# First 60 gathered u rows free of TensorE's pace, gate and spill loads issued from POOL

## The chip, the cores and the metric

One core of a Trainium2 chip runs the whole kernel in one launch. The metric is the device time of one execution in microseconds. Five engines take part: TensorE (PE in the profile, its weight loads PEld), VectorE (DVE), ScalarE (ACT), GpSimd (POOL) and SyncE (SP), which here only issues transfers.

## The reference

The model is two transformer blocks on 512 tokens of 1024 features in f32. The part that matters is the feed-forward layer of the first block's first layer, in which each token picks 8 x 16 = 128 of 16384 experts:

```python
def peer_ffn(x, w_q, sub_keys, u_emb, v_emb):
    ...
        eidx = jnp.take_along_axis(cidx, pos, axis=-1)      # 128 experts per token
        gate = jax.nn.softmax(top_s, axis=-1)
        u = u_emb[eidx]
        hid = jax.nn.gelu(jnp.einsum('td,thkd->thk', xc, u))
        wgt = (gate * hid.astype(jnp.float32)).astype(xc.dtype)
        return jnp.einsum('thk,thkd->td', wgt, v_emb[eidx])
```

`u_emb` and `v_emb` have 16384 rows of 1024 f32 numbers.

## The kernel before

TensorE multiplies f32 values as three products of halves: ScalarE rounds a weight tile to its high part (`uhi`, `vhi`, line 361) and VectorE subtracts to get the low part (`ulo`, `vlo`, line 362). SP loads the raw tile (`wraw`, 1 MB, line 351) into one of a few buffers, which comes free when both parts are made.

In layer 0 the 512 tokens are treated in two ways.

- The first 384 go through all 16384 experts. `select` and the routing pick the experts, `expand` makes a gate for every expert and token: VectorE builds one-hot tiles `ohA` (line 1512) and `ohB` (1514), TensorE multiplies them to `ps_g` (1527, 1528), and the gates go to DRAM (`gd`). There are 48 such steps, eight tokens each. Meanwhile TensorE computes hidden values `hs` of 42 of the 64 groups of 256 experts ahead of time, and stores them in DRAM (`hd`). Then the values stage runs 64 jobs, one per group: `prep` (1199) loads the gates G (line 1556, 768 KB, once for two jobs), loads `hs_r` from `hd` (line 1209, 384 KB) or computes it, multiplies both on VectorE (line 1213), and splits the product; `values` multiplies it by the v weights (`keep`, `ps_v`, line 1269), and VectorE adds `ps_v` into `racc` (1236). For 22 jobs the hidden values are computed here; they are interleaved in pairs with the jobs that load them, and 20 loading jobs come last.
- The last 128 tokens go through their own 128 experts each, in the class `Rows`. For each of 128 places POOL gathers one u row per token (`fetch`, line 258, an indirect transfer of a 128x1024 tile from a pool of 5), and VectorE multiplies it with the tokens and sums (the reduction, line 274: one instruction, and a short one that reads the sum). Then 128 gathers of v rows follow, each pair with small matmuls (`ps_row`).

What sets the order: `Rows.ticks` is a generator, and `spend` advances it by one tick for each `PACE` us of estimated matmul time that the code around it has emitted, times `rate` (`SLOW` within `expand`, 1 in the values stage). Tick p fetches row p and reduces row p-3. By `pace_by` a fetch waits on the chip for the last matmul emitted before it (`beat`), and the reduction is kept behind that matmul in the scheduler's order without a wait. The scheduler places each engine's instructions; on an engine they run in that order. POOL's queue has the fetches, an iota that `expand` reads, a copy (`glast`) and the first G load. SP's queue has the weights, and the other G and `hs_r` loads.

Of the kernel before, what the change touches and what calls it, by code (L numbers as in the profile page):

```python
# [46 lines left out]
PAY = ((2.9, 0.8), (5.0, 1.2))  # L47
NROW = 128
ROWBUFS = 5
PACE = (3.25, 3.1)  # L50
SLOW = 0.5
NPV = 4


# [154 lines left out]
class Rows:  # L209
# [21 lines left out]
    def begin(self, d1, d2, te):  # L231
# [10 lines left out]
        self.hid = pool.tile([P, P], F32, tag="hid", name="hid")  # L242
        self.steps, self.pace = self.ticks(), PACE[0]

# [11 lines left out]
    def fetch(self, name, idx):  # L256
        row = self.pool.tile([P, D], F32, tag="row", name="row", bufs=ROWBUFS)
        ins = self.nc.gpsimd.indirect_dma_start(row, None, self.p.g[name], bass.IndirectOffsetOnAxis(ap=idx, axis=0))  # L258
        self.pace_by(ins, mybir.DependencyClass.Sync)
        return row  # L260

    def pace_by(self, ins, kind):
# [3 lines left out]
    def ticks(self):  # L266
        nc, pool, prog = self.nc, self.pool, self.p
        rows = {}
        for p in range(P + 3):
            if p < P:  # L270
                rows[p] = self.fetch("urow", self.eu[:, p:p + 1])
            if p >= 3:
                row = rows.pop(p - 3)
                ins = nc.vector.tensor_tensor_reduce(out=row, in0=row, in1=self.xt, op0=ALU.mult, op1=ALU.add, scale=1.0, scalar=0.0,  # L274
                                                     accum_out=self.hid[:, p - 3:p - 2])
                self.pace_by(ins, mybir.DependencyClass.NoSync)
            yield
        self.pace = PACE[1]
        pt = prog.pm.tile([P, P], F32, tag="mm", name="ps_e")
        nc.tensor.transpose(pt, self.ef, prog.ident)  # L280
        self.ev = pool.tile([P, P], U32, tag="ev", name="ev")
        nc.vector.tensor_copy(self.ev, pt)
        nc.scalar.activation(self.hid, self.hid, AF.Gelu_apprx_tanh)
        nc.vector.tensor_tensor(self.hid, self.hid, self.gate, op=ALU.mult)
        order = [(r, i, g) for r in range(2) for i in range(32) for g in range(2)]
        ps = wt = None
        for n in range(P + 3):
            if n == 2:
                pt = prog.pm.tile([P, P], F32, tag="mm", name="ps_w")
                nc.tensor.transpose(pt, self.hid, prog.ident)  # L290
                wt = pool.tile([P, 2, 2, 32], F32, tag="wt", name="wt")
                nc.scalar.activation(wt.rearrange("p r g i -> p (r g i)"), pt, AF.Copy)
            if n < P:
                r, i, g = order[n]
                t = r * 64 + g * 32 + i
                rows[n] = self.fetch("vrow", self.ev[:, t:t + 1])
            if n >= 4 and n % 2 == 0:
                r, i, _ = order[n - 4]
                m = pool.tile([P, 2, 32], F32, tag="mask", name="mask2", bufs=4)
                nc.vector.tensor_tensor(m, self.hit[:, None, 31 - i:63 - i].to_broadcast([P, 2, 32]),  # L300
                                        wt[:, r, :, i:i + 1].to_broadcast([P, 2, 32]), op=ALU.mult)
                if i == 0:
                    ps = self.pv.tile([P, 512], F32, tag="rowv", name="ps_row")
                for h in range(2):
                    for g in range(2):
                        c = 32 * (2 * h + g)
                        nc.tensor.matmul(ps[c:c + 32, :], m[:, g, :], rows[n - 4 + g][:, h * 512:(h + 1) * 512],  # L307
                                         start=(i == 0), stop=(i == 31), tile_position=(0, c))
                del rows[n - 4], rows[n - 3]
                if i == 31:  # L310
                    self.add(r, ps)
            yield
# [17 lines left out]
class Prog:  # L330
# [869 lines left out]
    def prep(self, l, b, xh, xl, T, gd, hd):  # L1200

        nc = self.nc
        G = self.gates(l, b, gd, T // GSTAGE, T)
        hs = self.hsp.tile([P, 2, T], F32, tag="hs", name="hs_r", bufs=2)
        if b >= NLEAD[l]:
            for _ in self.hidden(l, b, xh, xl, T, hs):
                pass
        else:
            nc.sync.dma_start(hs, hd[b])
        Wh = self.pp.tile([P, 2, T], F32R, tag="Wh", name="Wh", bufs=2)  # L1210
        Wl = self.pp.tile([P, 2, T], F32R, tag="Wl", name="Wl", bufs=2)
        w = hs.rearrange("p j (q t) -> p j q t", t=GSTAGE)
        nc.vector.tensor_tensor(w, w, G.rearrange("p q j t -> p j q t"), op=ALU.mult)  # L1213
        self.split(Wh, Wl, hs)
        return Wh, Wl
# [279 lines left out]
    def expand(self, l, T, picks, gd):  # L1495

        nc = self.nc
        with self.tc.tile_pool(name=f"expand{l}", bufs=1, reuse_waits="tile") as kp:
# [6 lines left out]
            if self.rows:  # L1505
                self.rows.begun, self.rows.rate = True, SLOW
            for n in range(T // 8 + 1):
# [42 lines left out]
    def gates(self, l, b, gd, nq, T):  # L1550
        nc = self.nc
        key = (l, b // 2)
        if self.gcur is None or self.gcur[0] != key:
            G = self.pp.tile([P, nq, 4, GSTAGE], F32, tag="G", name="G", bufs=2)
            n = nq if self.gcur else nq - 1
            (nc.sync if self.gcur else nc.gpsimd).dma_start(G[:, :n].rearrange("p q j t -> p q (j t)"),
                              gd[:n, :, (b // 2) * 4:(b // 2) * 4 + 4, :].rearrange("q p j t -> p q (j t)"))
            if n < nq:
                nc.gpsimd.tensor_copy(G[:, n], self.glast)
            self.gcur = (key, G)  # L1560
        return self.gcur[1][:, :, (b % 2) * 2:(b % 2) * 2 + 2, :]
# [367 lines left out]
```

## Time and profile before

| | us |
|---|---|
| median of 3 runs | 3697.25 (3697.02 to 3698.64) |
| profiled execution | 3701.45, span 3699.7 |
| TensorE busy | 3574.0, granted clock 0.985 of full over the span |
| VectorE busy | 2461.5 |
| ScalarE busy | 1634.3 |
| POOL busy | 604.0 |
| u rows fetched | 975.9 to 1567.4 |
| v rows fetched | 1586.7 to 2079.5 |

Times in the trace count from the span's start. Selection and routing of layer 0 end with `expand`, which lies between some 957 and 1190 us; the values stage follows to some 2112 us. A mean share over the whole span says little here: the stretches have different engines near their limit, and the profile is read stretch by stretch.

### The profile page before, as it was taken

How to read it: one execution, taken by the hardware profiler on the slowest of the kernel's cores; microseconds unless marked ns; L12 is line 12 of the kernel's file. 1: busy time of each engine (PE TensorE's matmuls, PEld its weight loads, DVE VectorE, ACT ScalarE, POOL GpSimd, SP SyncE). 2: the span in 40 equal slices, each digit the busy share in tenths (PEclk: the TensorE clock that was granted, in tenths of full speed). 3: DMA queues.
4: the chain of work that ended last, by engine and by line, in shares of the span. 5: the costliest groups of instructions: out<-in, count | busy, mean ns of one | idle time of the engine just before them, and what ended most of it. 6: DMA issues, size and time to landing. Idle time of an engine off the chain costs nothing.

```text
span 3699.7 us, 55016 instructions
## 1 busy us (share of the span) xinstructions
PE 3574.0 (97%) x21681; PEld 3097.0 (84%) x21681; DVE 2461.5 (67%) x4540; ACT 1634.3 (44%) x2608; POOL 604.0 (16%) x686
## 2 busy tenths in 40 slices
PE   7999999899999998999999999999999999999999
PEld 5988877789999877776766799999998888887787
DVE  5566556599697777744445677778876555557675
ACT  3334333336576322222222354555676444445454
POOL 0112222100011232322222121221000000002121
PEclk9999999999999999999999999999999999999999
DMA  5222145224689898888889533354578766766453
GB/s 212 75 86 80 69 154 216 75 83 170 228 323 336 315 332 306 325 295 309 298 321 325 188 115 120 120 175 160 200 269 292 244 236 237 242 231 212 145 174 111
DMA packets 227763, 777.60 MB, mean 210 GB/s; under 512 B 17296, under 2 KB 100752, under 8 KB 168496
## 3 DMA queue, kind: packets, MB, share of 16 engines
q1 hardware_dynamic: 165984, 567.29, 43.7%
q0 software_dynamic: 37184, 135.41, 10.4%
q10 hardware_dynamic: 24336, 71.38, 5.0%
q8 instruction: 170, 2.79, 0.3%
q14 instruction: 89, 0.73, 0.1%
HBM read 705.60 MB, written 68.42 MB: 209 GB/s over the span
## 4 chain that ended last, share of the span: by engine, by line
PE 41%; DVE 4%; DMA 2%; ACT 1%; issue 1%; POOL 1%; DVEq 0%; ACTq 0%; SPq 0%; POOLq 0%
PE keep L1269 12%; PE ps_mm L393 5%; PE ps_mm L395 5%; PE ps_mm L394 5%; PE ps_wide L395 2%; PE ps_wide L393 2%; PE ps_wide L394 2%; PE ps_v L1269 1%; DVE ulo L362 1%; PE ps_nar L393 1%; PE ps_nar L395 1%; PE ps_nar L394 1%; DMA wraw<-in_v 1%; PE ps_mm L414 1%; PE ps_row L307 1%
## 5 line engine op out<-in xcount | busy, mean ns | idle before, releaser
L361 ACT ACTIVATE uhi<-wraw 128x1024 fp32r<-128x1024 f32 x586 | 609.0, 1057 | 879.2 <-PE ps_mm L394 336.1
L393 PE MATMUL ps_mm<-xh,uhi 128*128 128x256 f32 (+2 forms) x2952 | 955.5, 324 | 9.2 <-ACT hs L1566 3.7
L395 PE MATMUL ps_mm<-xh,ulo 128*128 128x256 f32 (+2 forms) x2952 | 940.8, 319 | 7.1 <-DVE ulo L362 7.1
L362 DVE TENSOR_TENSOR ulo<-wraw,uhi 128x1024 fp32r<-128x1024 f32 x586 | 718.0, 1237 | 340.6 <-ACT uhi L361 317.6
L394 PE MATMUL ps_mm<-xl,uhi 128*128 128x256 f32 (+2 forms) x2952 | 939.9, 318 | 0.0
L393 PEld LDWEIGHTS ps_mm<-xh,uhi 128*128 128x128 f32 x2952 | 562.5, 191 | 54.0 <-issue 9.2
L395 PEld LDWEIGHTS ps_mm<-xh,ulo 128*128 128x128 f32 x2952 | 562.2, 191 | 29.4 <-DVE ulo L362 8.0
L394 PEld LDWEIGHTS ps_mm<-xl,uhi 128*128 128x128 f32 x2952 | 562.7, 191 | 20.8
L362 DVE TENSOR_TENSOR vlo<-wraw,vhi 128x1024 fp32r<-128x1024 f32 x184 | 224.0, 1222 | 187.7 <-ACT vhi L361 187.5
L361 ACT ACTIVATE vhi<-wraw 128x1024 fp32r<-128x1024 f32 x184 | 193.2, 1056 | 338.1 <-DMA wraw<-in_v 176.0
L1269 PE MATMUL keep<-vlo,Wh 128*128 128x512 f32 x656 | 256.7, 391 | 3.6 <-DVE vlo L362 3.6
L1269 PE MATMUL keep<-vhi,Wh 128*128 128x512 f32 x656 | 257.8, 393 | 0.5 <-ACT Wh L422 0.5
L1269 PE MATMUL keep<-vhi,Wl 128*128 128x512 f32 x656 | 256.2, 391 | 0.3 <-DVE Wl L423 0.3
L258 POOL DMA_INDIRECT row<-in_urow,eu x128 | 158.5, 1238 | 589.7 <-PE ps_mm L395 440.7
L1213 DVE TENSOR_TENSOR hs_r<-hs_r,G 128x768 f32<-128x768 f32 (+1 forms) x128 | 105.2, 823 | 170.7 <-DMA hs_r<-hd 106.9
L393 PE MATMUL ps_nar<-uhi,xh 128*128 128x256 f32 x704 | 201.3, 286 | 2.3 <-ACT cs L664 2.3
L394 PE MATMUL ps_nar<-ulo,xh 128*128 128x256 f32 x704 | 200.1, 284 | 0.0
L395 PE MATMUL ps_nar<-uhi,xl 128*128 128x256 f32 x704 | 199.9, 284 | 0.0
L258 POOL DMA_INDIRECT row<-in_vrow,ev x128 | 136.0, 1063 | 375.4 <-PE keep L1269 180.2
L1530 ACT ACTIVATE stage<-ps_g 128x512 f32<-128x512 f32 x160 | 165.1, 1160 | 1.7 <-DMA wraw<-in_u 0.8
L274 DVE CUSTOM_DVE_ANT_0 row<-row,xt 128x1024 f32<-128x1024 f32 x128 | 155.2, 1219 | 4.5 <-DMA row<-in_urow,eu 4.5
L1269 PEld LDWEIGHTS keep<-vhi,Wh 128*128 128x128 f32 x656 | 123.7, 189 | 36.8 <-issue 9.2
(428 smaller groups left out, 6965.2 us busy)
## 6 DMA issues: line engine op xcount, KB each, us to landing
wraw<-in_u SPq DMA_DIRECT2D x128, 1024.0 KB
wraw<-in_v SPq DMA_DIRECT2D x128, 1024.0 KB
wraw<-in_wa SPq DMA_DIRECT2D x104, 1024.0 KB
wraw<-in_wb SPq DMA_DIRECT2D x50, 1024.0 KB
gd<-stage ACTq DMA_DIRECT2D x80, 512.0 KB
wraw_m<-in_wmod SPq DMA_DIRECT2D x24, 1024.0 KB
G<-gd SPq DMA_DIRECT2D x31, 768.0 KB
mraw<-in_wmod SPq DMA_DIRECT2D x16, 1024.0 KB
```

Source lines behind the costliest of these rows:

```text
L258: ins = self.nc.gpsimd.indirect_dma_start(row, None, self.p.g[name], bass.IndirectOffsetOnAxis(ap=idx, axis=0))
L274: ins = nc.vector.tensor_tensor_reduce(out=row, in0=row, in1=self.xt, op0=ALU.mult, op1=ALU.add, scale=1.0, scalar=0.0, accum_out=self.hid ...
L307: nc.tensor.matmul(ps[c:c + 32, :], m[:, g, :], rows[n - 4 + g][:, h * 512:(h + 1) * 512], start=(i == 0), stop=(i == 31), tile_position=( ...
L361: nc.scalar.activation(hi, r, AF.Copy)
L362: nc.vector.tensor_tensor(lo, r, hi.bitcast(F32), op=ALU.subtract)
L393: nc.tensor.matmul(ps, lh, rh, start=(i == 0), stop=False)
L394: nc.tensor.matmul(ps, lh, rl, start=False, stop=False)
L395: self.beat = nc.tensor.matmul(ps, ll, rh, start=False, stop=(i == n - 1))
L414: self.nc.tensor.matmul(ps[:, t0:t1], a[:, s], b[:, k, t0:t1], start=(n == 0 and i == 0), stop=(n == KD - 1 and i == 2))
L1213: nc.vector.tensor_tensor(w, w, G.rearrange("p q j t -> p j q t"), op=ALU.mult)
L1269: self.beat = self.nc.tensor.matmul(ps, a[:, j, t], b[:, c], start=(start and j == 0 and i == 0), stop=(stop and j == 1 and i == 2), skip_ ...
L1530: nc.scalar.activation(st[:, :, tb:tb + 4].rearrange("p j t -> p t j"), pg, AF.Copy, scale=1.0 / GSCALE)
```

## The change

The reductions and fetches of the first 60 ticks (`NFREE`) are no longer tied to a matmul: the fetch waits for its buffer and the indices alone, and the reduction may stand anywhere in VectorE's order. The pace is 3.45 us for u and 3.3 for v (3.25 and 3.1 before), and the rate in `expand` 0.7 (0.5 before). While `Rows` exists, which is in layer 0 only, all G and `hs_r` loads are issued by POOL.

```diff
--- before.py
+++ after.py
@@ -47,8 +47,9 @@
 PAY = ((2.9, 0.8), (5.0, 1.2))
 NROW = 128
 ROWBUFS = 5
-PACE = (3.25, 3.1)
-SLOW = 0.5
+PACE = (3.45, 3.3)
+SLOW = 0.7
+NFREE = 60
 NPV = 4
 
 
@@ -256,7 +257,8 @@
     def fetch(self, name, idx):
         row = self.pool.tile([P, D], F32, tag="row", name="row", bufs=ROWBUFS)
         ins = self.nc.gpsimd.indirect_dma_start(row, None, self.p.g[name], bass.IndirectOffsetOnAxis(ap=idx, axis=0))
-        self.pace_by(ins, mybir.DependencyClass.Sync)
+        if name == "vrow" or not self.free:
+            self.pace_by(ins, mybir.DependencyClass.Sync)
         return row
 
     def pace_by(self, ins, kind):
@@ -267,13 +269,15 @@
         nc, pool, prog = self.nc, self.pool, self.p
         rows = {}
         for p in range(P + 3):
+            self.free = p < NFREE
             if p < P:
                 rows[p] = self.fetch("urow", self.eu[:, p:p + 1])
             if p >= 3:
                 row = rows.pop(p - 3)
                 ins = nc.vector.tensor_tensor_reduce(out=row, in0=row, in1=self.xt, op0=ALU.mult, op1=ALU.add, scale=1.0, scalar=0.0,
                                                      accum_out=self.hid[:, p - 3:p - 2])
-                self.pace_by(ins, mybir.DependencyClass.NoSync)
+                if not self.free:
+                    self.pace_by(ins, mybir.DependencyClass.NoSync)
             yield
         self.pace = PACE[1]
         pt = prog.pm.tile([P, P], F32, tag="mm", name="ps_e")
@@ -1206,7 +1210,7 @@
             for _ in self.hidden(l, b, xh, xl, T, hs):
                 pass
         else:
-            nc.sync.dma_start(hs, hd[b])
+            (nc.gpsimd if self.rows else nc.sync).dma_start(hs, hd[b])
         Wh = self.pp.tile([P, 2, T], F32R, tag="Wh", name="Wh", bufs=2)
         Wl = self.pp.tile([P, 2, T], F32R, tag="Wl", name="Wl", bufs=2)
         w = hs.rearrange("p j (q t) -> p j q t", t=GSTAGE)
@@ -1553,7 +1557,7 @@
         if self.gcur is None or self.gcur[0] != key:
             G = self.pp.tile([P, nq, 4, GSTAGE], F32, tag="G", name="G", bufs=2)
             n = nq if self.gcur else nq - 1
-            (nc.sync if self.gcur else nc.gpsimd).dma_start(G[:, :n].rearrange("p q j t -> p q (j t)"),
+            (nc.sync if self.gcur and not self.rows else nc.gpsimd).dma_start(G[:, :n].rearrange("p q j t -> p q (j t)"),
                               gd[:n, :, (b // 2) * 4:(b // 2) * 4 + 4, :].rearrange("q p j t -> p q (j t)"))
             if n < nq:
                 nc.gpsimd.tensor_copy(G[:, n], self.glast)
```

The lines of the changed kernel stand 1 to 4 further down: line 258 becomes 259, 274 becomes 277, and from 284 on each is 4 more.

VectorE's order at the end of the routing and the start of `expand`, before (`picks` and `dec` are the routing's last results, `ulo` the low halves of weights for the hidden values):

```order
L1493 TENSOR_TENSOR dec_8737<-x 128x128
L1454 TENSOR_TENSOR te<-te,gsm 128x128
L362 TENSOR_TENSOR ulo<-wraw,uhi 128x1024 x7
L1512 TENSOR_TENSOR ohA<-io_8960,picks 128x2048
L1484 TENSOR_SCALAR picks<-ps_rt 128x16x8
L362 TENSOR_TENSOR ulo<-wraw,uhi 128x1024
L1485 SCALAR_TENSOR_TENSOR picks<-ps_rt,picks 128x16x8
L1514 TENSOR_TENSOR ohB<-ohA,picks 128x2048
L1512 TENSOR_TENSOR ohA<-io_8960,picks 128x2048
L362 TENSOR_TENSOR ulo<-wraw,uhi 128x1024
L1514 TENSOR_TENSOR ohB<-ohA,picks 128x2048
```

The same place now:

```order
L277 ISA hid 128x1
L277 ISA row,hid<-row,xt 128x1024
L277 ISA hid 128x1
L366 TENSOR_TENSOR ulo<-wraw,uhi 128x1024
L277 ISA row,hid<-row,xt 128x1024
L277 ISA hid 128x1
L277 ISA row,hid<-row,xt 128x1024
L277 ISA hid 128x1
L277 ISA row,hid<-row,xt 128x1024
L277 ISA hid 128x1
L366 TENSOR_TENSOR ulo<-wraw,uhi 128x1024
L1488 TENSOR_SCALAR picks<-ps_rt 128x16x8
```

Before, no reduction (`row,hid<-row,xt`) stands here; now they stand between the low halves, 24 of them above the first `ohA`, which follows behind the last row shown. Above the 25th `ohB` there are 55 reductions now and 12 before; the last of the 57 free ones stands above the 28th. TensorE's order in `expand` is the same in both.

POOL's order from `expand` into the values stage, before:

```order
L1501 IOTA io_8960 128x256
L258 DMA row<-in_urow,eu 128x1024 x30
L1542 COPY glast<-stage 128x128
L258 DMA row<-in_urow,eu 128x1024 x2
L1556 DMA G<-gd_6339 128x11x128
L1559 COPY G<-glast 128x128
L258 DMA row<-in_urow,eu 128x1024 x96
```

And now:

```order
L259 DMA row<-in_urow,eu 128x1024 x27
L1505 IOTA io_8960 128x256
L259 DMA row<-in_urow,eu 128x1024 x33
L1546 COPY glast<-stage 128x128
L1560 DMA G<-gd_6339 128x11x128
L1563 COPY G<-glast 128x128
L1560 DMA G<-gd_6339 128x12x128
L1213 DMA hs_r<-hd_6340 128x768
L1560 DMA G<-gd_6339 128x12x128
L1213 DMA hs_r<-hd_6340 128x768
L1560 DMA G<-gd_6339 128x12x128
L259 DMA row<-in_urow,eu 128x1024 x7
```

The iota has moved behind 27 fetches, 60 fetches instead of 32 precede the first G load, and G and `hs_r` loads stand between the later fetches, about one every four rows; they have left SP's order, in which the rest is unchanged but for one row.

## Rows read from the trace of the kernel before

**Rows 1.** Head of the page: busy us of each engine, share of the span, instructions.

```profile
PE 3574.0 (97%) x21681; PEld 3097.0 (84%) x21681; DVE 2461.5 (67%) x4540; ACT 1634.3 (44%) x2608; POOL 604.0 (16%) x686
```

**Rows 2.** Stretches: us, busy PE, PEld, DVE, ACT, POOL (x count), PEclk, DMA share, GB/s.

```profile
850.00:957.00 107.00, 107.00 (x622) 106.91 (x621) 87.74 (x318) 61.13 (x115) 0.00 (x0) 1.00 0.50 176
957.00:1075.00 118.00, 116.16 (x914) 112.20 (x913) 97.27 (x96) 78.95 (x92) 18.57 (x15) 1.00 0.80 288
1075.00:1190.00 115.00, 113.66 (x901) 109.77 (x900) 97.07 (x100) 77.64 (x91) 20.08 (x18) 1.00 0.90 324
1190.00:1600.00 410.00, 380.35 (x1817) 322.60 (x1816) 290.33 (x393) 122.28 (x150) 127.09 (x104) 0.96 0.87 317
1600.00:2112.00 512.00, 502.81 (x2502) 354.07 (x2501) 247.32 (x353) 137.02 (x163) 131.77 (x126) 0.99 0.84 298
```

**Rows 3.** The same stretches, only the u-row reductions (two instructions a row).

```profile
850.00:957.00 107.00, 0.00 (x0) 1.00 0.50 176
957.00:1075.00 118.00, 14.73 (x24) 1.00 0.80 288
...
1190.00:1600.00 410.00, 120.60 (x198) 0.96 0.87 317
```

**Rows 4.** Waits by engine, 1190 to 1600 us: total us, times, longest.

```profile
ACT uhi L361 <- DMA wraw<-in_v: 97.1, 12, 14.2
...
PEld ps_mm L393 <- DVE racc L1236: 22.2, 10, 4.9
...
DVE hs_r L1213 <- DMA hs_r<-hd: 14.1, 5, 4.1
...
DVE row L274 <- DMA row<-in_urow,eu: 4.5, 3, 2.4
```

**Rows 5.** Waits of SP's queue, 1190 to 1600 us.

```profile
SPq L351 <- DVE ulo L362: 75.9, 20, 9.2
...
SPq L1556 <- DVE hs_r L1213: 57.7, 9, 8.9
```

**Rows 6.** Timeline of one stall: start, duration, instruction, idle before and releaser.

```profile
1248.88 8.78 SPq L1556 DMA_DIRECT2D G<-gd  x2
1261.85 0.35 SPq L351 DMA_DIRECT2D wraw<-in_v  x1
...
1269.88 2.00 ACT L361 ACTIVATE uhi<-wraw 128x1024 fp32r<-128x1024 f32 x2 [9.23 <-DMA wraw<-in_v]
...
1270.97 2.36 DVE L362 TENSOR_TENSOR ulo<-wraw,uhi 128x1024 fp32r<-128x1024 f32 x2 [4.79 <-ACT uhi L361]
...
1273.98 0.69 PE L393 MATMUL ps_mm<-xh,vhi 128*128 128x384 f32 x1 [4.47 <-DVE racc L1236]
```

**Rows 7.** Timeline: eu, first ohB and ps_g, the 25th, two reductions.

```profile
850.43 0.21 DVE L238 CAST eu<-ef 128x128 uint32<-128x128 f32 x1
...
956.63 1.22 DVE L1514 TENSOR_TENSOR ohB<-ohA,picks 128x2048 f16<-128x2048 f16 x1
...
970.24 0.23 PE L1527 MATMUL ps_g<-ohB,ohA 128*128 128x128 f16 x1
...
1073.49 1.22 DVE L1514 TENSOR_TENSOR ohB<-ohA,picks 128x2048 f16<-128x2048 f16 x1
...
1075.74 0.23 PE L1527 MATMUL ps_g<-ohB,ohA 128*128 128x128 f16 x1
...
1263.81 1.22 DVE L274 CUSTOM_DVE_ANT_0 row<-row,xt 128x1024 f32<-128x1024 f32 x1
...
1264.95 1.22 DVE L274 CUSTOM_DVE_ANT_0 row<-row,xt 128x1024 f32<-128x1024 f32 x1
```

**Rows 8.** Instructions by line on POOL: times, shortest, median, longest ns.

```profile
L258 POOL DMA_INDIRECT row<-in_urow,eu x128: 932/1164/1977, 975.9 to 1567.4; - x128
...
L1556 POOL DMA_DIRECT2D G<-gd x2: 1067/1122/1176, 1190.3 to 2828.5; - x2
...
L1501 POOL IOTA io<- x2: 1514/1520/1525, 814.1 to 2591.9; 128x256 f16 x2
```

## The prediction, made before the changed kernel was run

> **What bounds the kernel now.** I read the head of the page first: TensorE is busy 3574.0 us, 97% of the span of 3699.7, so only its idle time and its slow-clock time can be won or lost [rows 1]. Then the table of stretches shows where that time lies [rows 2]. From 850 to 1190 us (selection of experts, then `expand`) TensorE is busy 336.8 of 340 us at a granted clock of 1.00: nothing to win. In the first part of the values stage (1190 to 1600, where u rows are taken) it idles 410 - 380.35 = 29.7 us, and the granted clock is 0.96 of full, of 2.4 GHz; (1 - 0.96) x 410 = 16.4 us goes to slower matmuls. Together that is 46 us. In the second part (1600 to 2112, v rows) it is 9.2 + (1 - 0.99) x 512 = 14.3 us. No more than about 60 us, 1.6% of the run, is to be had.
>
> The table of waits for the first part says how the 46 us arise [rows 4]: TensorE waits for VectorE's `racc`, ScalarE's `uhi` waits 97.1 us for weight transfers and VectorE waits behind it. One cycle shows it [rows 6]: the weights issued at 1261.85 and 1262.29 us reach ScalarE at 1269.88 (9.23 us idle, ended by DMA), VectorE starts two `ulo` at 1270.97 (4.79 idle), `racc` comes behind them, and TensorE resumes at 1273.98 after 4.47 us. VectorE works in order, so whatever stands ahead of `racc` delays it, the reductions of u rows too. The u part has them, 198 instructions or 99 rows, and VectorE is busy 290 of 410 us; the v part has none, VectorE is busy 247 of 512, and the loss per us is a quarter [rows 2, 3].
>
> **The change part by part.**
>
> *Free rows, the loss.* The reductions of the first 57 rows are no longer ordered behind a matmul (the reduction runs three ticks behind the fetch, so 60 free ticks free 57 of them), and the scheduler has put them early. Counted in the order of VectorE: above the 25th `ohB` stand 12 reductions before and 55 now; above the first `ohA`, 0 and 24. The second figure for before agrees with the trace, which has no reduction up to 957 us and 24 instructions, 12 rows, up to 1075 [rows 3]. The 25th `ohB` runs at 1073.49 and ends at 1074.71; the `ps_g` matmuls that read it begin at 1075.74 [rows 7]. The slack is 1.0 us. Two reductions back to back are 1264.95 - 1263.81 = 1.14 us apart [rows 7], so 43 more cost 49 us of VectorE. From 850 us, when the row indices `eu` are made [rows 7], to 1075 VectorE is idle 225 - 185.0 = 40 us [rows 2]. If every idle piece is filled, the 25th `ohB` is late by 49 - 40 - 1.0 = 8 us, and TensorE with it. If only half of the idle time between 957 and 1075 can be used (20.7 us, in pieces between `ohA`, `ohB` and `ulo`), it is 18 us. TensorE's order is unchanged, and it is bound in both halves, so the delay isn't given back there. I take 13, the middle; ends 8 and 19. Row transfers could add to it: the share of the DMA engines up to 957 is 0.50, and up to 1075 0.80 [rows 2], and the five row buffers hold the queue to rows already reduced; that is why I don't take 8.
>
> *Free rows, the gain.* 28 fewer reductions and row fetches stand in the u part (71 of 99 left). In proportion the 46 us fall by 46 x 28/99 = 13. The ends: 5, if the late weights would be late without rows, and 35, if the whole stretch came down to the v part's loss of 14.3/512 per us, 11.5 us.
>
> *Pace.* 3.45 for 3.25 spreads the other 71 rows by 6%: of the remaining 33 us, 2. The v rows too are 6% further apart; their stage loses 14 us in all, so at most 1. At the end the last v rows come later, still ahead of the last jobs in the order: nothing.
>
> *Gate and spill loads.* 31 loads of G and 42 of `hs_r` leave SP's queue for POOL's. What they free on SP: it stood at G until VectorE's `hs_r` was done for 57.7 us in nine waits, in the u part [rows 5]. But in the cycle of rows 6 SP is free of G at 1248.88 + 8.78 = 1257.7 and issues the weights only at 1261.85; the wait of SP's weight issues for `ulo`, 75.9 us, is the longer one [rows 5]. So most of this hold hides behind the raw buffer. I take 3 us of gain, with ends 0 and 15 (a third of the 46).
>
> The share of the DMA engines in the u part is 0.87 at 317 GB/s [rows 2], whichever queue issues. The Trainium skill (Trainium Kernel Development and Optimization, Key Constraints) says that transfers issued by SP, ACT and POOL share the same 16 DMA engines and that several issuers save only issue time; by it this term is about 0. The Trainium skill (DMA: Bandwidth & Descriptors, Queues, rings and completion order) also says that each DMA engine takes turns between the queues it has work for; by that the weights no longer stand behind G in their ring, and the term would lie towards 15. The row on SP's waits and the row on the weight issue lie nearer to the first.
>
> What they cost on POOL: a G there took 1.07 to 1.18 us, a row fetch about as long [rows 8]. 73 x 1.12 = 82 us more, beside 127.1 + 131.8 busy in 922 us [rows 2]: 37% in use, no bound. Queued behind a G that waits for VectorE are the row fetches. They are given three ticks, 3 x 3.45 = 10.4 us, before their use, and in the u part VectorE waited for rows only three times, 4.5 us [rows 4]. The spill load now stands behind row fetches that wait for a matmul, but those are matmuls of an earlier job; VectorE waited 14.1 us for `hs_r` in this part [rows 4]. I take 0 for all this; its ends are 0, since it only lengthens a queue, and +18 (case D below).
>
> *The index table.* The iota of `expand` now stands behind 27 fetches. It took 1.52 us [rows 8]. The 27th fetch needs the buffer of row 22, and `ohA` stands behind 24 reductions: two reductions, 2.3 us, cover it. Without that cover 1.5 us.
>
> Sum against the profiled run of 3701.45 us (span 3699.7): +13 - 13 - 2 - 3 = -5, so 3696.5. That run is 4.2 us above the median of the runs, 3697.25, so the forecast is 3692 on the median's footing. Two sizeable terms nearly cancel.
>
> **The rivals.**
>
> *A, the forecast.* VectorE's backlog in `expand` costs about what the emptier u part returns: 3692, with 3682 to 3702 its own range. A measurement of this kernel tells about 0.2%, 7.4 us, from no change, so this case falls mostly under no change.
>
> *B, the cover holds.* The early rows fill all of VectorE's idle time and late weights vanish with the rows: loss 8, gain 20 + 2 + 8: -22, 3675. For it: VectorE and DMA have their only slack at 850 to 957 [rows 2], and rows sit on the stalled engine. Against: the wait that starts each stall is for weights, which stay.
>
> *C, the slower side: VectorE in `expand`.* Place: the `ohB` between 957 and 1120 us. Price: 19 us of delay, and if TensorE's gaps there pull down its granted clock as in the u part (16.4 us of clock loss to 29.7 of gaps [rows 2]), up to 10 more. With the gain at 15: +8 to +14, 3705 to 3711. It decides from the point where less than about 30 of the 40 idle us can be filled. For it: the slack of 1.0 us, and TensorE waiting for nothing of note there today. Against: the first `ohB` has over 10 us of slack, since it ends before 958 and TensorE reaches `ps_g` at 970 [rows 7].
>
> *D, POOL's line.* G waits on POOL for VectorE as it did on SP (57.7 us in nine waits in the u part [rows 5]), and rows behind it arrive late. If each of the nine took 2 us from TensorE, which is 18, the forecast would become 3692 + 18 = 3710. Against: the slack of 10 us per row.
>
> **How the numbers follow.** A has 0.50, B 0.20, C 0.22, D 0.08. Of A, a third lies beyond 7.4 us to the fast side (0.17), the rest within (0.33). Faster: 0.17 + 0.20 = 0.37. The same: 0.33. Slower: C and D, 0.30. The range runs from B, 3675, to the upper end of C, 3711: what is outside, a gain near 35 us or a loss with both C and D, has less than 2 in 10.
>
> **What would show it.** Right: TensorE gets idle time between 950 and 1120 us ended by `ohB` or `ulo`, 8 to 19 us of it, with VectorE near 100% busy there; the stretch from 1190 to the last u reduction is shorter and holds 25 to 33 us of loss instead of 46; no reduction for the first 30 us of the values stage; SP no longer stops at G. Wrong: TensorE unbroken to 1190 (B); granted clock below 0.95 in `expand` (C); TensorE idle ended by rows, or POOL standing at G for over 10 us at a time (D).

## The result: 42 us slower

| | us |
|---|---|
| before, 4 runs beside it | 3697.94 (3697.02 to 3702.35) |
| changed, 4 runs | 3739.84 (3737.29 to 3745.08) |
| ratio | 1.0113, 95% interval 1.0095 to 1.0130 |
| changed, profiled run | 3742.17, span 3740.3 |

The ratios here and below are taken over all runs of both kernels and can differ in the last digits from the quotient of two medians.

Where the time goes is read at instructions that both kernels have. `expand` ends with its last `ps_g` matmul, at 1180.5 us before and at 1198.4 now (operation and count, shortest, median and longest ns, first and last start):

```profile
L1528 PE MATMUL ps_g<-ohB,ohA x384: 218/218/221, 970.3 to 1180.5; 128*128 128x128 f16 x192
```

```profile
L1532 PE MATMUL ps_g<-ohB,ohA x384: 218/218/308, 976.7 to 1198.4; 128*128 128x128 f16 x192
```

For the end of the u part (the part of the values stage in which u rows are taken) I use the 865th of the 2364 matmuls on v weights. Before, after, and in the first experiment below, which has the free rows but not the moved loads:

```profile
1603.51 0.39 PE L1269 MATMUL keep<-vhi,Wh 128*128 128x512 f32 x1
```

```profile
1622.33 0.39 PE L1273 MATMUL keep<-vhi,Wh 128*128 128x512 f32 x1
```

```profile
1605.16 0.39 PE L1273 MATMUL keep<-vhi,Wh 128*128 128x512 f32 x1
```

So `expand` ends 17.9 us later, the u part 18.8 us later, and the whole stage, as is shown below, 43.7 us later. The stretches that follow are cut near these points, to within some 6 us. The columns are again the stretch, its length, the busy time (and count) of TensorE, its weight loads, VectorE, ScalarE and POOL, the granted clock, the share of the DMA engines and GB/s.

```profile
850.00:957.00 107.00, 106.37 (x617) 105.96 (x616) 101.50 (x345) 60.56 (x114) 30.88 (x22) 1.00 0.73 262
957.00:1075.00 118.00, 105.29 (x777) 100.57 (x776) 111.23 (x132) 66.66 (x78) 56.66 (x36) 0.93 0.92 346
1075.00:1208.00 133.00, 131.14 (x1041) 126.55 (x1040) 97.75 (x90) 90.06 (x105) 8.45 (x7) 1.00 0.75 281
1208.00:1613.00 405.00, 375.20 (x1807) 314.90 (x1806) 257.24 (x338) 120.68 (x148) 119.36 (x103) 0.96 0.80 286
1613.00:2156.00 543.00, 518.74 (x2514) 361.76 (x2513) 248.43 (x352) 139.53 (x166) 167.18 (x168) 0.98 0.78 277
```

Up to 957 us almost nothing is lost (0.6 us). Between 957 and 1075 us TensorE idles 118 - 105.3 = 12.7 us and its clock is 0.93 of full, (1 - 0.93) x 118 = 8.3 us, where before it was 1.8 us in all. The two overlap, since the clock is low in part while TensorE idles (about 3 of the 8 us); that is why their sum of 21 is more than the 17.9 us by which `expand` ends later. The u part has as much idle time and slow clock as before (30 and 16 us). The v part takes 25 to 31 us more than before, by the one cut or the other: 24.3 us idle and 2% of clock, against 9.2 and 1%.

A matmul that ends the layer, after its last wait for POOL's `rst`, shows the delay of the whole stage. Before, and then after:

```profile
2117.26 0.58 PE L475 MATMUL ps_y<-ident,rst 128*128 128x128 f32 x1 [1.06 <-POOL rst L470]
```

```profile
2160.97 0.58 PE L479 MATMUL ps_y<-ident,rst 128*128 128x128 f32 x1 [1.06 <-POOL rst L474]
```

2160.97 - 2117.26 = 43.7 us; the spans differ by 40.6, since layer 1 gives some back.

The loss at the start of `expand` is at VectorE and at one place. Its timeline (start, duration, instruction, idle before and what ended it):

```profile
987.02 1.22 DVE L277 CUSTOM_DVE_ANT_0 row<-row,xt 128x1024 f32<-128x1024 f32 x1 [1.83 <-DMA row<-in_urow,eu]
...
989.31 1.22 DVE L1516 TENSOR_TENSOR ohA<-io,picks 128x2048 f16<-128x2048 f16 x1
990.45 1.22 DVE L277 CUSTOM_DVE_ANT_0 row<-row,xt 128x1024 f32<-128x1024 f32 x1
...
991.59 1.22 DVE L1518 TENSOR_TENSOR ohB<-ohA,picks 128x2048 f16<-128x2048 f16 x1
```

And TensorE's:

```profile
992.87 0.29 PE L1531 MATMUL ps_g<-ohB,ohA 128*128 128x128 f16 x1 [5.71 <-DVE ohB L1518]
...
997.42 0.29 PE L1531 MATMUL ps_g<-ohB,ohA 128*128 128x128 f16 x1 [2.66 <-DVE ohB L1518]
```

The reductions stand between `ohA` and `ohB`, one waits 1.83 us for its row, and TensorE waits 5.71 and 2.66 us for `ohB`. The `ohB` at 991.59 is the third of `expand`. Before it ran here:

```profile
973.75 1.23 DVE L1514 TENSOR_TENSOR ohB<-ohA,picks 128x2048 f16<-128x2048 f16 x1
```

It is 17.8 us late, with 31 reductions above it where there were none. They are not the whole of it: from 940 to 990 us VectorE also stood for rows that had not landed (total, times, longest):

```profile
DVE row L277 <- DMA row<-in_urow,eu: 10.9, 7, 4.4
```

TensorE's third step of `ps_g` begins 12.3 us later than before (992.87 against 980.56), the seventh 17.8 (1015.51 against 997.73) and the 25th 17.8 (1093.59 against 1075.74). So the order of VectorE did foretell a backlog, but all of the delay is made in the first seven steps; the reductions that follow up to the 25th `ohB` cost nothing more.

The loss of the v part has another place. The waits from 1613 to 2156 us (total, times, longest):

```profile
DVE hs_r L1217 <- DMA hs_r<-hd: 128.1, 26, 12.3
...
POOL G L1560 <- DVE hs_r L1217: 44.6, 11, 8.4
POOL hs_r L1213 <- DVE Wl L427: 35.8, 11, 10.2
PEld ps_row L311 <- DMA row<-in_vrow,ev: 33.7, 13, 5.6
```

TensorE's matmuls on v rows (`ps_row`) wait for the rows; its weight loads show it for 33.7 us in 13 waits. POOL stands 44.6 us at G and 35.8 at `hs_r`, and VectorE 128.1 us for `hs_r`.

### The profile page after: what moved, and what is told of

The parts are those of the page before. It is cut to its first block, busy times and chain, and to the rows that moved or that the text cites. A ratio compares the mean times of both kernels' runs of the same rounds, so it can differ in the third digit from the quotient of the medians.

```text
span 3740.3 us, 55041 instructions
## 1 busy us (share of the span) xinstructions
PE 3585.5 (96%) x21681; PEld 3096.6 (83%) x21681; DVE 2457.3 (66%) x4540; ACT 1635.5 (44%) x2608; POOL 686.6 (18%) x759
## 4 chain that ended last, share of the span: by engine, by line
PE 56%; DVE 7%; DMA 7%; issue 6%; POOL 3%; ACT 2%; ACTq 0%; POOLq 0%; DVEq 0%; SPq 0%
PE keep L1273 13%; PE ps_mm L397 8%; PE ps_mm L399 8%; PE ps_mm L398 8%; PE ps_v L1273 2%; DMA wraw<-in_v 2%; DVE ulo L366 2%; DMA hs_r<-hd 2%; PE ps_wide L399 2%; PE ps_wide L397 2%; PE ps_wide L398 2%; DMA row<-in_vrow,ev 2%; PE ps_row L311 1%; POOL row L259 1%; PE ps_mm L418 1%
## 5 line engine op out<-in xcount | busy, mean ns | idle before, releaser
L259 POOL DMA_INDIRECT row<-in_urow,eu x128 | 180.6, 1411 | 447.7 <-issue 165.1
L426 ACT ACTIVATE Wh<-hs_r 128x768 fp32r<-128x768 f32 (+1 forms) x128 | 93.2, 728 | 145.1 <-DVE hs_r L1217 68.5
```

Of the source, the lines that this page charges most:

```text
L426: nc.scalar.activation(hi, src, AF.Copy)
```

## The experiments

Four kernels first split the change into its parts.

**Free rows without the moved loads.** The changed kernel, with two lines put back:

```diff
-            (nc.gpsimd if self.rows else nc.sync).dma_start(hs, hd[b])
+            nc.sync.dma_start(hs, hd[b])
-            (nc.sync if self.gcur and not self.rows else nc.gpsimd)
+            (nc.sync if self.gcur else nc.gpsimd)
```

> The changed kernel with all gate and spill loads back on SP; the 60 free rows and the new pace stay. Theory Q (the loads make POOL's line of row fetches late, which costs TensorE some 30 us in the v part and eats the gain of the u part): the 18 us lost at the start of expand stay, the v part is as before the change, 3698 to 3708. Rival P (the v rows' slower pace and later end cause the v part's loss): about 3730 to 3740, as the changed kernel.

Measured 3694.45 against 3696.32, ratio 0.9992 (0.9982 to 1.0001), a little below what I expected. Two stretches of this run:

```profile
957.00:1075.00 118.00, 105.46 (x777) 100.62 (x776) 111.46 (x134) 66.90 (x81) 58.16 (x36) 0.94 0.93 346
...
1208.00:1596.00 388.00, 369.40 (x1811) 312.95 (x1810) 257.48 (x338) 121.88 (x149) 95.29 (x78) 0.98 0.83 299
```

In `expand` the loss is that of the changed kernel (105.5 busy, clock 0.94; its last `ps_g` starts at 1199.0, 18.5 us later than before). At the 865th matmul only 1.7 us of it are left, so the u part returns 17 us, and the layer ends 4.6 us earlier than before (the `ps_y` above at 2112.68). So the free rows, with the new pace and rate, cost about 18 us in one place and return about 23 in the next two. The whole of the slowdown is with the loads.

**The moved loads alone.** The changed kernel with `PACE = (3.25, 3.1)`, `SLOW = 0.5` and `NFREE = 0`.

> The kernel before with only the gate and spill loads moved to POOL; pace, rate and row order as before. Theory Q: 3720 to 3735, with TensorE waiting for v rows as in the changed kernel, and nothing lost in expand. Rival P: 3690 to 3700.

Measured 3749.14 against 3696.32, 1.0137 (1.0119 to 1.0155): 53 us, more than expected. Its stretches:

```profile
957.00:1190.00 233.00, 229.78 (x1811) 221.93 (x1811) 193.59 (x195) 157.14 (x184) 39.76 (x34) 1.00 0.86 306
1190.00:1612.00 422.00, 379.22 (x1797) 321.30 (x1796) 288.98 (x392) 119.59 (x147) 148.20 (x126) 0.94 0.85 307
1612.00:2167.00 555.00, 521.09 (x2519) 359.55 (x2518) 247.32 (x353) 139.07 (x165) 171.65 (x175) 0.97 0.77 276
```

`expand` is untouched (233 us as before), the u part takes some 12 us more and the v part some 43.

**The pace alone.** `NFREE = 0` and the loads on SP, with the new pace and rate.

> The kernel before with only the new pace (3.45 and 3.3) and rate in expand (0.7). Theory Q: 3688 to 3700; the rate takes some 12 rows into expand, evenly, at no loss there. Rival P: 3720 to 3730, with TensorE waiting for v rows.

Measured 3698.4, 1.0001 (0.9988 to 1.0015). Rival P falls: v rows further apart cost nothing. The expectation "no loss in expand" was wrong, though. TensorE's idle time is 4 us between 957 and 1075 and 5 us from there to 1190, and `expand` ends 11.7 us later than before, more than half of what the free rows lose; by the 865th matmul 6.4 us of it are left, and by the `ps_y` 3.2. Its last `ps_g`, and two waits from 957 to 1192 us:

```profile
L1532 PE MATMUL ps_g<-ohB,ohA x384: 218/218/308, 970.8 to 1192.2; 128*128 128x128 f16 x192
```

```profile
ACT uhi L365 <- DMA wraw<-in_u: 15.3, 4, 4.8
...
PE ps_g L1531 <- ACT stage L1534: 8.7, 10, 2.5
```

Here TensorE waits 8.7 us for ScalarE's copies of the gates (`stage`; 3.1 us before, from 957 to 1190) and only 0.4 for `ohB`, and ScalarE waits 15.3 us for weights (3.6 before). So the 18 us of the free rows can't be put down to them alone: they contain the higher rate, which alone costs 11.7 by another wait. How the 18 divide isn't shown.

**G alone, and the spill loads alone,** each on the changed kernel, the other load back on SP.

> The changed kernel with the spill loads (hs_r) back on SP, only G on POOL. If it is G that stops POOL's line (it waits there for VectorE's product, 6 to 10 us at a time): 3730 to 3740. If the spill loads do it: 3705 to 3715. If both add up: about 3720. Rival P: 3735 to 3745.

> The changed kernel with G back on SP, only the spill loads (hs_r) on POOL. G alone on POOL cost some 12 us beside the free rows (3706.8 against 3694.5). If the two costs add up, the spill loads cost the other 33: 3725 to 3731. If only both together make the loop (G waits for the product of a late spill load, rows wait for G): 3700 to 3710.

G alone: 3706.82 against 3696.32, 1.0031 (1.0018 to 1.0044). Spill loads alone: 3704.66 against 3697.92, 1.0016 (1.0007 to 1.0025). Over the free rows, which stand at -1.9, that is 12 and 9 us; both together are 41.9 + 1.9 = 44. They don't add up to 21: only the two together cost most of it. By the first expectation 3706.82 would have meant that the spill loads do it; they alone cost 9 us, so none of its cases holds. The last case of the second does.

Then three kernels, built on the kernel before, ask what it is about POOL.

**The waits without the bytes.** POOL writes one column of each buffer, and SP then loads it:

```diff
+            if self.rows:
+                nc.gpsimd.memset(hs[:, 0, :1], 0.0)
             nc.sync.dma_start(hs, hd[b])
...
+            if self.gcur and self.rows:
+                nc.gpsimd.memset(G[:, 0, 0, :1], 0.0)
```

> The kernel before, its loads on SP; POOL writes one column of each hs_r buffer and each G buffer (not the first) before SP loads it. So POOL waits for the same buffers in the same places as with the loads on it, and SP's load follows POOL's write, but no byte of the loads goes through POOL's queue. Theory W (POOL's in-order line stands at those waits, and rows and loads behind it are issued late): 3735 to 3750, as with the loads moved. Rival B (bytes and descriptors of the loads ahead of the rows in the same queue): 3695 to 3708.

Measured 3695.84 against 3697.92, 0.9997 (0.9987 to 1.0006): no cost. Its waits from 1600 to 2130 us:

```profile
DVE hs_r L1215 <- DMA hs_r<-hd: 60.4, 21, 7.1
...
POOL hs_r L1210 <- DVE Wl L423: 49.1, 16, 9.5
...
POOL G L1559 <- DVE hs_r L1215: 32.4, 12, 4.8
...
PEld ps_row L307 <- DMA row<-in_vrow,ev: 4.5, 4, 1.9
```

POOL stands at the two writes for 49.1 + 32.4 us, about as long as at the loads of the changed kernel (35.8 + 44.6), with row fetches queued behind them, and TensorE waits 4.5 us for rows. My theory W falls: standing in line is, by itself, not the cost.

**Few bytes and half the bytes.** POOL issues a part of each load, SP the rest. The small part (`src` is the source of G; SP's loads of the rest of G are left out here):

```diff
+                nc.gpsimd.dma_start(hs[:, 0, :128], hd[b][:, 0, :128])
+                nc.sync.dma_start(hs[:, 0, 128:], hd[b][:, 0, 128:])
+                nc.sync.dma_start(hs[:, 1, :], hd[b][:, 1, :])
...
+                nc.gpsimd.dma_start(G[:, 0, 0, :], src[0, :, 0, :])
```

The half has `hs[:, 0, :]` and `G[:, :6]` on POOL and the other halves on SP.

> The kernel before; of each hs_r load POOL issues one sixth (65 KB), of each G (not the first) one part in 48 (16 KB), SP the rest. POOL issues as many transfers as in the version with all loads on it, with the same waits, but few bytes. Theory B (bytes ahead of the rows and of each other in the one queue that POOL feeds): 3695 to 3708. [...]

> The same with half the bytes of each load issued by POOL and half by SP. Theory B, if the cost grows with the bytes and each load half shortens the other: between 3703 and 3725. [...]

Small: 3708.31 against 3698.9, 1.0029 (1.0015 to 1.0043). Half: 3720.2, 1.0056 (1.0039 to 1.0073). In one table, with the bytes that POOL issues in 73 loads (42 x 64 + 31 x 16 KB, 42 x 192 + 31 x 384, 42 x 384 + 31 x 768), and two waits from 1600 to 2130 us: VectorE's for `hs_r`, and that of TensorE's weight loads for v rows. The two single loads are counted over the free rows:

| on POOL | MB | us over the base | wait for `hs_r` | wait for rows |
|---|---|---|---|---|
| kernel before | 0 | 0 | 70.2 | 1.8 |
| waits only | 0 | -2 | 60.4 | 4.5 |
| small part | 3.3 | +9 | 113.7 | 5.9 |
| half | 20 | +21 | 132.3 | 16.5 |
| all | 41 | +53 | 124.4 | 39.9 |
| `hs_r` alone | 17 | +9 | 72.5 | 2.9 |
| G alone | 24 | +12 | 102.4 | 4.1 |

Where parts of both loads are on POOL the cost grows with the bytes. The bytes are not the only thing that counts: 24 MB of G alone cost 12 us and 20 MB of both 21. The number of transfers isn't the main thing either, since POOL issues as many in the small version as with all loads on it. The small version lies at the upper edge of what theory B expected, and there SP also issues one more transfer per load; its rows are hardly late (5.9 us), its `hs_r` is (113.7). Whether these 9 us are the price of more transfers the runs don't separate. Rows are late by more than 6 us in all only with half or all of both loads on POOL.

How the bytes may do it is seen in one place of the version with only the loads moved, in the v part, where TensorE's longest wait for a row stands. POOL's timeline:

```profile
1927.69 1.08 POOL L1560 DMA_DIRECT2D G<-gd  x1 [4.14 <-DVE ulo L366]
1929.07 0.97 POOL L259 DMA_INDIRECT row<-in_vrow,ev  x1 [0.30 <-issue]
1930.35 1.44 POOL L259 DMA_INDIRECT row<-in_vrow,ev  x1 [0.30 <-issue]
1932.14 0.59 POOL L1213 DMA_DIRECT2D hs_r<-hd  x1 [0.35 <-DVE Wl L427]
1933.03 0.96 POOL L259 DMA_INDIRECT row<-in_vrow,ev  x1 [0.30 <-issue]
1934.30 0.94 POOL L259 DMA_INDIRECT row<-in_vrow,ev  x1 [0.30 <-issue]
1948.90 0.58 POOL L1213 DMA_DIRECT2D hs_r<-hd  x1 [13.67 <-DVE Wl L427]
```

VectorE's and TensorE's in the same stretch:

```profile
1944.36 0.96 DVE L1217 TENSOR_TENSOR hs_r<-hs_r,G 128x768 f32<-128x768 f32 x1 [11.24 <-DMA hs_r<-hd]
...
1947.65 0.95 DVE L427 TENSOR_TENSOR Wl<-hs_r,Wh 128x768 fp32r<-128x768 f32 x1
```

```profile
1942.22 1.08 PE L311 MATMUL ps_row<-row,mask 128*32 128x512 f32 x3 [10.17 <-DMA row<-in_vrow,ev]
```

And stretches of 4 and 5 us, columns as above:

```profile
1927.00:1932.00 5.00, 5.00 (x20) 3.16 (x19) 5.00 (x7) 0.00 (x0) 3.49 (x3) 1.00 0.50 113
1932.00:1936.00 4.00, 0.05 (x1) 0.00 (x0) 1.11 (x2) 0.00 (x0) 2.48 (x3) 0.79 0.96 358
1936.00:1940.00 4.00, 0.00 (x0) 0.00 (x0) 0.00 (x0) 0.00 (x0) 0.00 (x0) 0.50 1.02 414
1940.00:1944.00 4.00, 1.78 (x6) 0.19 (x6) 0.00 (x0) 0.00 (x0) 0.00 (x0) 0.50 0.99 394
1944.00:1948.00 4.00, 4.00 (x17) 2.03 (x14) 2.65 (x5) 0.84 (x1) 0.00 (x0) 0.50 0.11 44
```

G waits 4.14 us for VectorE, and then a G, two rows, an `hs_r` and two more rows are issued within 8 us, 768 + 384 + 4 x 512 KB, and SP issues a weight tile at 1933.01. From 1932 to 1944 us the DMA engines are full (0.96 to 1.02 of their time), and TensorE and VectorE stand: TensorE 10.17 us for a row, VectorE 11.24 us for the `hs_r` issued at 1932.14. When both have landed, at 1944 us, the DMA engines are nearly empty (0.11): the next `hs_r` waits at POOL for VectorE's `Wl` (13.67 us), the next rows wait behind it, and SP issues its next weight tile only at 1948.56. A group like this one stands before it: a G, a row, an `hs_r` and two rows from 1904.84 to 1910.17, with the DMA engines at 0.99 to 1.04 from 1908 to 1920 and at 0.30 in the 4 us after. After 1948.90 the loads and rows are issued further apart, and TensorE doesn't stop up to 1964.

I read a loop of four links in it: late loads, late product on VectorE, late issue on POOL, late rows and loads. With G or `hs_r` alone on POOL the lump is smaller, and with waits alone the loads run in SP's queue beside the rows; that this breaks the loop is my reading of the table. TensorE's granted clock falls to half, 1.2 GHz, in the stall (0.50 from 1936 to 1948 us).

That the lump is what hurts is read from this stretch and from the table, and is not shown: no run took the lump away with the bytes kept.

**The loads on ScalarE.**

```diff
+            (nc.scalar if self.rows else nc.sync).dma_start(hs, hd[b])
```

G alike.

> The kernel before with the same loads issued by ScalarE instead of POOL or SP, so that their bytes stand neither ahead of the rows nor ahead of the weights. What the weights gain from it is the term that the prediction put at 3 us (0 to 15): 3688 to 3697. If ScalarE's stops at these loads delay the weights' high parts: 3700 to 3720.

Measured 3716.47 against 3698.9, 1.0047 (1.0028 to 1.0065). The loads stand in the queue of neither rows nor weights, and it is still 18 us slower. The rows are not late here (3.4 us from 1600 to 2130), but `hs_r` is (109.7 us, 70.2 before). This leaves a rival open: a part of the 53 us, up to these 18, may come from the loads leaving SP's queue, whichever queue takes them. This kernel doesn't separate that, nor what an emptier SP queue gives, from what ScalarE's own stops at the loads cost. Whether the weights gain is seen in their landing times, in the page's table of DMA issues (count, KB, median us to landing, over both layers). Loads on SP (free rows alone):

```profile
wraw<-in_u SPq DMA_DIRECT2D x128, 1024.0 KB, 5.8
wraw<-in_v SPq DMA_DIRECT2D x128, 1024.0 KB, 5.5
...
row<-in_vrow,ev POOLq DMA_INDIRECT x128, 6.9
```

The changed kernel:

```profile
wraw<-in_u SPq DMA_DIRECT2D x128, 1024.0 KB, 6.0
wraw<-in_v SPq DMA_DIRECT2D x128, 1024.0 KB, 5.9
...
row<-in_vrow,ev POOLq DMA_INDIRECT x128, 7.5
```

With G and `hs_r` gone from SP's queue the weights land no sooner (6.0 and 5.9 against 5.8 and 5.5), and the rows later (7.5 against 6.9). Layer 1, which the change leaves alone, is in the weights' medians; in the values stage alone (issues from 1208 us on) they are 7.7 against 7.6.

**A version that keeps `expand` whole.** Loads on SP, the new pace, and:

```diff
-SLOW = 0.7
-NFREE = 60
+SLOW = 0.5
+NFREE = 20
...
                 self.rows.begun, self.rows.rate = True, SLOW
+                self.rows.due = NFREE * PACE[0]
```

> A version meant to beat both: loads on SP, 20 free ticks due at once when expand begins, after them the rate 0.5 of before in expand, and the new pace. 17 reductions stand above the first ohA, the others are spread over expand as before. If VectorE's full order in expand was the 18 us of the free rows: no more than 3 us lost there, and the u part still 8 to 14 us shorter: 3684 to 3691. If any early row costs in expand: 3693 to 3702.

Measured 3691.48 against 3697.92, 0.9982 (0.9973 to 0.9992): faster than before by 6 us, half a us above what I expected. Its `expand`:

```profile
957.00:1190.00 233.00, 229.79 (x1812) 221.94 (x1812) 198.59 (x202) 156.51 (x183) 35.58 (x31) 1.00 0.86 307
```

`expand` is as before (229.8 of 233 busy, clock 1.00, as in [rows 2]); 17 reductions lie before the first `ohA`, in idle time, and 31 above the 25th `ohB`. Where the 6 us come from the trace doesn't show: in the profiled run the 865th matmul of the values stage is 2.3 us later than before, and the `ps_y` that ends the layer 2.5 us earlier (2114.78 against 2117.26). The u part is not the 8 to 14 us shorter that I expected.

**Four rows more.** The same with `NFREE = 24`, `SLOW = 0.55` and the v pace of before.

> As the version with 20 free ticks due at once, but with 24, the rate 0.55 in expand and the v pace of before (3.45 and 3.1). If the loss in expand starts only where VectorE's reductions exceed its idle time there: within 3 us of no loss in expand, and 3685 to 3692 in all. If 24 rows ahead of the first ohA are already too many: 5 to 8 us lost in expand and 3692 to 3698.

Measured 3698.73 against 3697.17, 1.0002 (0.9993 to 1.0011). In its profiled run TensorE loses about 2 us in `expand`, within the 3 that I expected of idle time not yet exceeded, but the time lies above both of my ranges, and the gain of the other version is gone from the median. I didn't find out whether the pace or the four rows took it.

## Why the prediction was wrong

- *What bounds the kernel, and where:* right. All changes lie in `expand` and the values stage, and each was traced from TensorE's waits.
- *Free rows, the loss in `expand`:* right about the engine and nearly about the size, 18 us where I took 13 with ends 8 and 19; the place within `expand` was wrong. I summed up to the 25th `ohB` and its slack of 1.0 us. The delay is made by the third, 17.8 us late, and is whole at the seventh step. VectorE's 10.9 us of standing for rows are in it, which I had named without a price, and so is the new rate, which alone delays `expand` by 11.7 us, with ScalarE waiting for weights; the sum had no term for that. That the size came out near is partly luck. The clock's share, which I had put into case C only, is up to 8 us of it; C's sign, a granted clock below 0.95 in `expand`, came true. (C's lower end is a slip: 19 us with no clock loss and a gain of 15 give +4, not +8.)
- *Free rows, the gain in the u part, with the pace:* right in sign, 17 us where I took 13 + 2, and 6 more in the v part, where I took nothing. Of the 17, 12 are back by the matmul that starts at 1303.2 us before (6.6 us late there): no row at all is reduced at the start of the values stage now, which a gain in proportion to the rows leaves out. Free rows and pace came to 13 - 13 - 2 = -2 in the sum, and to -1.9 on the chip. That agreement is luck: the loss and the gain were both taken too small.
- *Gate and spill loads, the gain on SP:* no sign of the 3 us that I took. The reading that SP's stop at G hides behind the raw buffer was right; the Trainium skill's rule (Trainium Kernel Development and Optimization, Key Constraints) that several issuers save only issue time fits the landing times, 6.0 and 5.9 us against 5.8 and 5.5. It says nothing of what the move costs.
- *Gate and spill loads, the cost on POOL:* the step that failed. "I take 0 for all this; its ends are 0, since it only lengthens a queue, and +18" measured 44 us on the free rows and 53 alone. I added up POOL's time, 37% in use, and looked at each load's own slack, 10 us a row. Neither is the limit. What I missed is that 73 loads of 41 MB stand among 196 row fetches in POOL's line, one for every 2.7 of them (not one for every four, as I had counted), and that with both kinds there rows and `hs_r` land late: TensorE's weight loads waited 33.7 us for v rows in the changed kernel, VectorE 128.1 us for `hs_r`. That they are issued in lumps, since VectorE's product, which ends POOL's waits, waits for the same transfers, is my explanation; how the cost arises link by link stays open. In case D the place was right and the reason wrong: the wait in line alone is free (-2 us), and D's price of 18 us was too low.
- *The iota:* no wait for it is seen in the changed kernel's waits from 957 us on; 0.
- *The signs to look for:* the first held (TensorE idle ended by `ohB`, VectorE 94% busy from 957 to 1075 us). The loss of 25 to 33 us in the u part held with the free rows alone (18.6 us idle, 7.8 of clock), not in the changed kernel (46). The one for D, TensorE idle ended by rows, is what decided; POOL stood at G for 9.8 us at most, just under the 10 that I had named.

## What to carry to other kernels

Before moving transfers to another engine's queue, draw the loop: who ends the wait of that engine, and does that one wait for the same transfers? A slack that is enough for each transfer alone says nothing of a lump in which they are all issued at once. And work that is moved into an engine's idle time is free only up to the idle time ahead of the next instruction that others wait for, and only if its data are there: 17 reductions ahead of the first `ohA` and 31 by the 25th `ohB` cost nothing, while with 24 ahead of `ohA` and 31 by the third `ohB`, at the higher rate, `expand` lost 18 us.

## What the runs showed that I had not expected

The DMA engines went from 0.99 of their time to 0.11 from one stretch of 4 us to the next, with a mean of 0.77 over the v part of the version with the loads moved. The mean share, lower than before (0.84 in [rows 2]), would have looked like relief.
